# Two decoder layers on one core: routing in two steps, small products in turn, stage seams in quarters

## The chip, the core and the metric

The kernel runs on one core of one Trainium2 chip. A core has five engines, each with its own queue of instructions that it works through in order: TensorE (PE; its loading of the stationary operand is listed apart as PEld), VectorE (DVE), ScalarE (ACT), GpSimd (POOL) and SyncE (SP), which here mostly issues DMAs. They work at the same time and wait for each other through semaphores. TensorE writes to PSUM (banks of 128 x 512 fp32 words); the other data lies in SBUF. The metric is the device time of one execution in microseconds (us), median of several; less is better.

## The reference, cut to what matters

Two consecutive layers of a decoder, one sequence of 256 tokens, width 1024, all in float32:

```
for layer in range(2):
    h = rmsnorm(x, norm1[layer])
    x = x + hybrid_mixer(h, ...)          # proj = h @ w_in; three groups of heads; concat @ w_out
    h = rmsnorm(x, norm2[layer])
    if layer == 0:
        x = x + (silu(h @ ffn_gate) * (h @ ffn_up)) @ ffn_down           # inner width 2816
    else:
        probs = softmax(h @ router)                                      # 8 experts
        top_p, top_i = top_k(probs, 2); top_p /= sum(top_p)
        for e in range(8):
            x += gate[:, e] * swiglu(h, w_gate[e], w_up[e], w_down[e])    # inner width 1536
```

The mixer has three parts side by side: gated DeltaNet (6 heads of 64; a causal convolution, then a recurrence over 4 chunks of 64 tokens that carries a 64 x 64 state per head), forgetting attention (6 heads of 64; softmax attention with a cumulated log decay), and a pooling part of 4 groups with windows of 2 to 16 tokens. In RMSNorm each token is scaled by one positive number, r = 1/sqrt(mean(x^2) + eps), and each channel by a gain.

## The kernel before

**Products.** Every large product is made of three products of fp32r operands: a float32 is split in a high part and the rest, and the sum is hi·hi + hi·lo + lo·hi (`mm3`). `hi_lo` makes the parts: ACT copies the high part (recorded at L238), DVE subtracts (L241). All matmuls are recorded at L244, transposes at their own lines (L361 those of the norm, named `pst`).

**Weights.** `piece` (L283) issues the load of a piece of weights (up to 128 x 1152) on SyncE's queue into a ring of 6 raw buffers (more in the experts' stage), and splits it into one of 4 pairs `whi`, `wlo`. Splits run ahead of their use, as far as these buffers allow. In each stage pieces 2 to 5 are held behind the last split of the norm by a dependency (`self.split_h`), so that the norm's splits come first.

**Stages.** `mixer` of layer 0, `dense`, `mixer` of layer 1, `moe`; a stage begins with `norm` (L346), which multiplies by the gain (`xn`), transposes 8 blocks of 128 x 128 per token tile through four `pst` banks (one pair of PSUM tag F for the first token tile, one of tag D for the second), and splits them into `hThi`, `hTlo`. The factor r isn't applied there: it is worked out beside (four squares on ACT, then Ln, Exp and a Newton step on DVE, buffer `nt`) and multiplied in later. PSUM tags A, D, F have 3, 3, 2 banks in the mixers, 4, 2, 2 in dense, 2, 4, 2 in moe.

**The mixer's small products.** The DeltaNet part makes two Gram matrices per 128 tokens (`gram`, PSUM name `ps_KK`), solves a triangular system (`delta_solve`, `ps_j`), and runs over the four chunks (`delta_scan`): `ps_ks` and `ps_v` for the new values, `ps_S` for the state, and into `ps_o` the output, from the state S (128 x 128 per pair of heads) and from the matrix P (64 x 64 per head). A product of 64 x 64 uses a quarter of the array: the row half by the partitions of its operands (here the chunk), the column half by those of its result. `log_decays` (`ps_c`) turns columns into rows, `attention` sums P·V per head into `ps_fo`.

**The ends of mixer and dense.** The last product of a mixer, `ps_out`, has four quarters (two token tiles by two column halves), each a PSUM bank: three of tag A and then one of tag F. Rows 0 to 4 run as their weights come; rows 5 to 7 are kept, and run quarter by quarter, each followed by its addition to `xs`. In `dense`, a step f makes 128 inner columns of gate and up (`ps_gu`) and adds the down product of the step before (`ps_dn`, four banks); the last two are kept and run quarter by quarter, both of a quarter together, each quarter followed by its addition to `xs` (L975).

**Routing and experts.** `route` (L978) multiplies `hThi`, `hTlo` with the router (`ps_ro`), copies the result (`rt`), folds hi and lo (`ps_lg`), scales by r, forms the softmax, ranks each token's experts by two comparisons with a rule for ties, selects those of rank under 2 (`sel`), and counts each token's place with its expert (`ps_pos`). `experts` (L1109) then fills expert 0's 0/1 matrix `disp` by comparing places with numbers (`fill`), gathers its tokens from `xh` and `xl` (the parts of `xn`, made by ACT and by POOL at L1307) as products with `disp` (`ps_ga`), and goes on to gates, `places` (L1033: the order of the other experts by their load, read by SyncE into registers at L1064, since it sets the address of each load), the other fills, and `slots` (L1090, `ps_slot`: each slot's gate, token and r). Then 32 steps, 8 experts by 4 quarters of the inner width: `gate_up` (`ps_e`), silu with r as its scale (`info`), and one step later `down` (`ps_y`). Three lightly loaded experts ("small") have 64 slots, and their hi and lo parts share one operand; their last two k blocks use the raw float32 weights. `finish` splits an expert's sum, `scatter` adds it to `xs`. `store` issues one DMA per token tile. If an expert overflows its slots, the experts run again for the rest; with these inputs this doesn't happen.

**Order.** The program is written with the Tile framework, whose planner puts each engine's instructions in order by priorities: loads and splits have AHEAD = 2000 over the rest, the norm and the routing twice that. Within an engine the order is then fixed.

Of the kernel before, what the change touches and what calls it, by code (L numbers as in the profile page):

```python
# [16 lines left out]
F32 = mybir.dt.float32  # L17
F32R = mybir.dt.float32r
# [7 lines left out]
D = 1024  # L26
# [59 lines left out]
def shape_constants():  # L86
# [29 lines left out]
    r.add("iota", np.broadcast_to(np.arange(256.0), (128, 256)))  # L116
    r.add("lt", np.broadcast_to((e[None, :] < e[:, None]).reshape(1, 64), (128, 64)))
    r.add("room", np.broadcast_to(np.isin(e, SMALL) * 64.0, (128, 8)))
# [27 lines left out]
def pack(inputs):  # L146
# [30 lines left out]
    out["cst"], out["rcst"] = cst.array(), rcst.array()  # L177
    PAR_AT["cst"], PAR_AT["rcst"] = cst.at, rcst.at
# [8 lines left out]
ORDER = ("x", "gains", "cst", "rcst", "par0", "par1", "win", "wout", "ffn", "moe")  # L187


class Kernel:  # L190
# [92 lines left out]
    def piece(self, ap):  # L283
# [23 lines left out]
    def setup(self):  # L307
# [4 lines left out]
        self.par = [cp.tile([128, self.d[f"par{l}"].shape[1]], F32, name=f"par{l}t") for l in range(2)]  # L312
# [32 lines left out]
    def norm(self, along=True):  # L345
# [7 lines left out]
        for t in range(2):  # L353
# [9 lines left out]
            xn.append(x)  # L363
        ss = self.sm.tile([128, 4], F32, tag="ss", name="ss")
# [6 lines left out]
        nc.vector.tensor_scalar(v, ss[:, 0:2], 1.0 / D, EPS, op0=ALU.mult, op1=ALU.add)  # L371
# [11 lines left out]
        return xn, hi, lo  # L383


    def proj_tokens(self, g, hi, lo):
# [5 lines left out]
        for (k0, k1), (wh, wl) in zip(cuts, ws):  # L392
            for t in range(2):
                tk = slice(t * 128, t * 128 + 128)
                for k in range(k0, k1):
                    s = slice((k - k0) * n, (k - k0 + 1) * n)
                    self.mm3(ps[t][:, :n], hi[:, k, tk], lo[:, k, tk], wh[:, s], wl[:, s], k == 0, k == 7)
# [148 lines left out]
    def delta_keys(self, kq):  # L546
# [42 lines left out]
        for hp in range(3):  # L589
            ps = self.psF("ps_eGb")  # L590
            for t in range(2):
                self.mm(ps[:, t * 128:t * 128 + 128], ex[t][:, 2 * hp:2 * hp + 2].rearrange("p a d -> p (a d)"), self.ident)
            self.copy(eGb[:, hp], ps[:, :T])
# [14 lines left out]
    def gram(self, kq, s, dest, tag):  # L608

        for t in range(2):  # L610
            for h2 in range(2):
                ps = self.ps(tag, "ps_KK")
                r = slice(h2 * 64, h2 * 64 + 64)
                for m in range(3):
                    for c in range(2):
                        n = slice((2 * t + c) * 64, (2 * t + c) * 64 + 64)
# [732 lines left out]
```

## Time and profile before

| | |
|---|---|
| median of 3 runs | 986.93 us (986.68 to 988.48) |
| profiled execution | 987.85 us |
| its span | 986.1 us |
| mean granted TensorE clock | 0.973 |
| moved by DMA | 224.78 MB, mean 228 GB/s |

The span runs from the first to the last instruction in the records; the execution's time has 1.75 us more around it. The stages by their first and last product: mixer 0 to 167.4, dense 171.5 to about 356.6, mixer 1 to 519.5, then routing and experts to the end.

The page gives the busy time of each engine over the span, then the chain that ended last, followed back from the last instruction to whatever released each step. The rows of groups give line, engine, operation, result <- operands by the program's names, partitions x elements and type, and a count; then the busy time, the mean of one in ns, and the idle time of the engine just before them with what ended it. Rows of the timeline start with the time in us from the span's start and the duration; `x4` means four such instructions in a row, taken together. The granted clock (PEclk) is that which the throttle let TensorE have, as a share of full speed. Matmuls overlap: the next starts before the end that is drawn for the last.

### The profile page before, as it was taken

To read this page: it belongs to the slowest core of one execution; us is meant where nothing else is said; L and a number is where in the kernel's file an instruction comes from. 1 tells how busy PE (TensorE), PEld (TensorE's weight loads), DVE (VectorE), ACT (ScalarE), POOL (GpSimd) and SP (SyncE) were. 2 spreads that over 40 slices of the span, in tenths; PEclk is the share of its full clock that TensorE was granted. 3 is DMA by queue.
4 is the path that set the end of the run, shared out by engine and by line. 5 is a ranking of instruction groups with operands and counts; after the bars stand their busy time and mean duration, and the time that the engine had idled before them with its cause. 6 is when DMAs were issued, how large, how long until landed. Compare 5 with 4: busy or idle time off the path is not lost.

```text
span 986.1 us, 17576 instructions
## 1 busy us (share of the span) xinstructions
PE 923.9 (94%) x6483; PEld 823.7 (84%) x6483; DVE 734.8 (75%) x1036; ACT 623.7 (63%) x987; POOL 131.1 (13%) x196
## 2 busy tenths in 40 slices
PE   6988998999999989889994999999999899999996
PEld 6887776999999989788773999987889788998874
DVE  6877657655555568767558587998899898998895
ACT  6754545544444457555535388876887688877773
POOL 2696100000000023881002000000000000000000
PEclk9999999999999989989997799999999999999999
DMA  9533113666666646342134399999999999998991
GB/s 355 169 90 126 45 44 132 213 194 183 187 189 190 174 127 194 107 129 67 41 131 182 98 348 325 364 364 352 374 366 376 358 337 351 391 342 316 330 405 50
DMA packets 61983, 224.78 MB, mean 228 GB/s; under 512 B 6896, under 2 KB 7152, under 8 KB 61888
## 3 DMA queue, kind: packets, MB, share of 16 engines
q1 hardware_dynamic: 61344, 221.62, 64.7%
q0 software_dynamic: 544, 1.94, 0.5%
q8 instruction: 53, 0.87, 0.4%
q14 instruction: 42, 0.34, 0.1%
HBM read 222.49 MB, written 1.05 MB: 227 GB/s over the span
## 4 chain that ended last, share of the span: by engine, by line
PE 75%; DVE 8%; POOL 6%; DMA 5%; ACT 3%; issue 2%; SPq 0%; DVEq 0%; ACTq 0%; POOLq 0%
PE ps_e L244 23%; PE ps_gu L244 13%; PE ps_y L244 11%; PE ps_dn L244 6%; PE ps_out L244 4%; DMA raw<-moe 3%; DVE wlo L241 3%; PE ps_fq L244 3%; PE ps_ga L244 2%; PE ps_o L244 1%; POOL cacc L514 1%; PE ps_p L244 1%; ACT whi L238 1%; POOL U L576 1%; DVE cacc L518 1%
## 5 line engine op out<-in xcount | busy, mean ns | idle before, releaser
L241 DVE TENSOR_TENSOR wlo<-raw,whi 128x1024 fp32r<-128x1024 f32 (+3 forms) x394 | 478.4, 1240 | 138.2 <-ACT whi L238 135.1
L238 ACT ACTIVATE whi<-raw 128x1024 fp32r<-128x1024 f32 (+3 forms) x394 | 412.3, 1066 | 181.2 <-PE ps_e L244 53.7
L244 PE MATMUL ps_e<-wlo,gThi 128*128 128x384 f32 x464 | 161.9, 349 | 4.5 <-DVE wlo L241 4.4
L244 PE MATMUL ps_e<-whi,gThi 128*128 128x384 f32 x464 | 157.8, 346 | 1.2 <-ACT whi L238 1.2
L244 PE MATMUL ps_e<-whi,gTlo 128*128 128x384 f32 x320 | 109.0, 342 | 0.0
L244 PE MATMUL ps_gu<-hThi,whi 128*128 128x256 f32 x352 | 99.1, 282 | 1.3 <-DVE hTlo L241 1.3
L244 PE MATMUL ps_gu<-hTlo,whi 128*128 128x256 f32 x352 | 98.7, 280 | 0.0
L244 PE MATMUL ps_gu<-hThi,wlo 128*128 128x256 f32 x352 | 98.7, 280 | 0.0
L244 PEld LDWEIGHTS ps_e<-wlo,gThi 128*128 128x128 f32 x464 | 89.3, 193 | 9.7 <-DVE wlo L241 6.9
L244 PEld LDWEIGHTS ps_e<-whi,gThi 128*128 128x128 f32 x464 | 88.9, 192 | 4.6 <-ACT whi L238 1.6
L244 PE MATMUL ps_y<-wlo,ehi 128*128 128x512 f32 x192 | 73.4, 401 | 1.0 <-DVE wlo L241 1.0
L244 PEld LDWEIGHTS ps_gu<-hThi,whi 128*128 128x128 f32 x352 | 66.1, 188 | 2.5 <-DVE hTlo L241 1.5
L244 PEld LDWEIGHTS ps_gu<-hThi,wlo 128*128 128x128 f32 x352 | 67.4, 191 | 0.0
L244 PE MATMUL ps_y<-whi,ehi 128*128 128x512 f32 x192 | 65.9, 408 | 1.3 <-DVE ehi L241 1.3
L244 PEld LDWEIGHTS ps_gu<-hTlo,whi 128*128 128x128 f32 x352 | 66.1, 188 | 0.8
L244 PEld LDWEIGHTS ps_e<-whi,gTlo 128*128 128x128 f32 x320 | 61.6, 193 | 0.6
L244 PE MATMUL ps_y<-whi,elo 128*128 128x512 f32 x120 | 46.6, 392 | 0.0
L244 PEld LDWEIGHTS ps_y<-whi,ehi 128*128 128x128 f32 x192 | 36.3, 191 | 9.8 <-DVE ehi L241 2.1
L244 PEld LDWEIGHTS ps_y<-wlo,ehi 128*128 128x128 f32 x192 | 36.2, 190 | 9.3 <-DVE wlo L241 1.8
L244 PE MATMUL ps_e<-raw,gThi 128*128 128x384 f32 x96 | 36.2, 500 | 0.0
L244 PE MATMUL ps_dn<-whi,fhi 128*128 128x512 f32 x88 | 34.4, 391 | 0.1
L244 PE MATMUL ps_dn<-wlo,fhi 128*128 128x512 f32 x88 | 34.3, 389 | 0.0
(394 smaller groups left out, 1794.1 us busy)
## 6 DMA issues: line engine op xcount, KB each, us to landing
raw<-moe SPq DMA_DIRECT2D x128, 576.0 KB, 6.2
raw<-moe SPq DMA_DIRECT2D x96, 512.0 KB, 6.1
raw<-ffn SPq DMA_DIRECT2D x66, 512.0 KB, 3.5
raw<-moe SPq DMA_DIRECT2D x64, 384.0 KB, 5.9
raw<-win SPq DMA_DIRECT2D x34, 512.0 KB, 3.8
raw<-wout SPq DMA_DIRECT2D x16, 512.0 KB, 3.5
raw<-win SPq DMA_DIRECT2D x8, 402.0 KB, 5.1
raw<-win SPq DMA_DIRECT2D x4, 576.0 KB, 4.5
```

The costliest lines, as they stand in the source:

```text
L238: return self.nc.scalar.activation(out, in_, AF.Copy, scale=scale)
L241: return self.nc.vector.tensor_tensor(out, a, b, op=op)
L244: self.nc.tensor.matmul(out, l, r, start=start, stop=stop)
L514: eng.tensor_scalar(acc, x, w[:, o + 3:o + 4], None, op0=ALU.mult)
L518: nc.vector.scalar_tensor_tensor(acc[:, j:], x[:, :T - j], wj, acc[:, j:], op0=ALU.mult, op1=ALU.add)
L576: nc.gpsimd.tensor_tensor(u, u, tv, op=ALU.subtract)
```

## The change

**Routing in two steps.** The order of a token's logits doesn't depend on its r, so the selection now works on the raw logits: one subtraction, one comparison with a constant that holds the rule for ties. r (`factor`), the softmax and expert 0's scale `first` are issued after the products of step 0, the gates (`shares`), `places`, the other fills, `slots` and the parts `xh`, `xl` after those of step 1 (`then`). `xl` moves from POOL to DVE. Expert 0 is gathered from `xn` in float32 and the sum is split (`gather_whole`); its last two k blocks use the float32 operand `g6` and raw weights. `slots` works with fp32r products (6 columns: parts of gate and r, and the token). A table `self.after` says behind what the first five splits of a stage stand: in moe the first two behind the last split of the norm, the next three behind the copy of `rt` (ACT) and the first fill (DVE). The routing's constants are loaded a stage earlier into the buffer of `par0`, by POOL's queue.

```diff
@@ piece
-        if 1 < self.pieces < 6:
-            for i, last in zip(parts, self.split_h):
+        if self.pieces < 6:
+            for i, last in zip(parts, self.after[min(self.pieces, 3)]):
                 self.dep(i, last)
@@ route
-        lg = sm.tile([128, 2, NE], F32, name="lg", bufs=1)
-        self.tt(lg, ps[:, :16].rearrange("p (t e) -> p t e", t=2), self.r[:, :, None].to_broadcast([128, 2, NE]), ALU.mult)
...
+        raw = sm.tile([128, 2, NE], F32, name="lraw", bufs=1)
+        nc.vector.tensor_copy(raw.rearrange("p t e -> p (t e)"), ps[:, :16])
+
         c1 = sm.tile([128, 2, NE, NE], F32, name="c1", bufs=1)
-        c2 = sm.tile([128, 2, NE, NE], F32, name="c2", bufs=1)
-        self.tt(c2, others, mine, ALU.is_equal)
-        self.tt(c1, others, mine, ALU.is_gt)
-        lower = self.rc("lt").rearrange("p (a b) -> p a b", b=NE)[:, None].to_broadcast([128, 2, NE, NE])
-        self.tt(c2, c2, lower, ALU.mult)
-        self.tt(c1, c1, c2, ALU.add)
+        self.tt(c1, raw[:, :, None, :].to_broadcast([128, 2, NE, NE]), raw[:, :, :, None].to_broadcast([128, 2, NE, NE]), ALU.subtract)
+        self.tt(c1, c1, self.rc("tie").rearrange("p (a b) -> p a b", b=NE)[:, None].to_broadcast([128, 2, NE, NE]), ALU.is_gt)
@@ slots
+        for i, v in ((0, gr), (2, r)):
+            nc.vector.tensor_copy(gt[:, :, :, i], v)
+            self.tt(gt[:, :, :, i + 3], v, gt[:, :, :, i].bitcast(F32), ALU.subtract)
...
-                self.mm(ps[:, 3 * e:3 * e + 3], P[t][:, e].bitcast(F32), gt[:, t, e], t == 0, t == 1)
+                self.mm(ps[:, 6 * e:6 * e + 6], P[t][:, e], gt[:, t, e], t == 0, t == 1)
@@ experts
+        def gather_whole():
+
+            g = [self.big.tile([128, 8, 1, 128], F32R, tag=x, name="g" + x) for x in ("Thi", "Tlo")]
+            g.append(wk.tile([128, 2, 128], F32, name="g6", bufs=1))
+            for k in range(0, 8, 4):
+                ps = self.psF("ps_ga")
+                for i in range(4):
+                    for t in range(2):
+                        self.mm(ps[:, i * 128:i * 128 + 128], xn[t][:, (k + i) * 128:(k + i + 1) * 128], P[t][:, 0].bitcast(F32), t == 0, t == 1)
+                self.gathered = self.hi_lo(g[0][:, k:k + 4, 0], g[1][:, k:k + 4, 0], ps.rearrange("p (k c) -> p k c", k=4))
+            self.copy(g[2].rearrange("p k c -> p (k c)"), ps[:, 256:])
+            return g
...
-            self.act(sg, ga, AF.Silu, scale=info[0][:r, p, 2:3])
+            self.act(sg, ga, AF.Silu, scale=first if len(g) == 3 else info[0][:r, p, 2:3])
...
+                self.after[3] = self.rt_copy, filled
+                g[0] = gather_whole()
+
+        def factors():
+
+            nonlocal first
+            begun = self.factor(False)
+            self.dep(begun, self.gathered[1])
+            r2 = wk.tile([128, 2, 2], F32R, name="r2", bufs=1)
+            nc.vector.tensor_copy(r2[:, :, 0], self.r)
+            self.tt(r2[:, :, 1], self.r, r2[:, :, 0].bitcast(F32), ALU.subtract)
+            ps = self.psF("ps_first")
+            for t in range(2):
+                self.mm(ps[:, :2], P[t][:, 0], r2[:, t], t == 0, t == 1)
+            first = wk.tile([128, 1], F32, name="first", bufs=1)
+            self.first_known = nc.vector.tensor_reduce(first, ps[:, :2], axis=AX.X, op=ALU.add)
+            self.softmax()
+            self.tables("silu_and_others")
+
+        def rest_of_routing():
+            nonlocal info
+            begun = [self.shares(), self.places()]
+            fill(slice(1, 6, 2), 128)
...
+            info = self.slots(P)
+            for t in range(2):
+                self.dep(self.hi_lo(xh[t], xl[t], xn[t])[1], self.slots_known)
+            for i in begun:
+                self.dep(i, self.first_known)
```

**Seams.** `proj_tokens` and the first step of `dense` issue all products with `hThi` first, those with `hTlo` after. The quarters of `ps_out` take the banks F, A, A, A instead of A, A, A, F, so that the quarter that closes first holds the bank of tag F. In `dense` the row before the last runs over all four quarters first, then the last one quarter by quarter with the addition to `xs`. The result is stored in four DMAs.

```diff
@@ mixer
-        po = [self.ps("AAAF"[i], f"ps_out{i}") for i in range(4)]
+        po = [self.ps("FAAA"[i], f"ps_out{i}") for i in range(4)]
@@ dense
+        (f0, h0), (f1, h1) = late
         for t in range(2):
             for e in range(2):
-                for f, h in late:
-                    rows(f, t, e, *h)
+                rows(f0, t, e, *h0)
+        for t in range(2):
+            for e in range(2):
+                rows(f1, t, e, *h1)
                 x = self.xs[t][:, e * 512:e * 512 + 512]
```

**Small products in turn.** Products that use different parts of the array are issued alternately: in `gram` over both heads of a pair and both chunks, in `delta_scan` the output products of both chunks of a token tile together (they were issued with each chunk), in `log_decays` over both heads of a pair, in `attention` `ps_fo` once per pair of heads. The three products with the identity for `eGb` become transposes.

```diff
@@ delta_scan
-            for m in range(3):
-                if S is not None:
-                    self.mm(po[r, m * 128:m * 128 + 128], self.qd[:, m, ns], S[:, m], True, False)
-                for h in (2 * m, 2 * m + 1):
-                    self.mm(po[r, h * 64:h * 64 + 64], self.P[r, t * 6 + h], src[r, h], S is None, S is None or h % 2 == 1)
+            states.append(S)
+            if c == 1:
+
+                both = [(c, slice(c * 64, c * 64 + 64), states[2 * t + c]) for c in range(2)]
+                for m in range(3):
+                    for c, r, S0 in both:
+                        if S0 is not None:
+                            ns = slice((2 * t + c) * 64, (2 * t + c) * 64 + 64)
+                            self.mm(po[r, m * 128:m * 128 + 128], self.qd[:, m, ns], S0[:, m], True, False)
+                    for h in (2 * m, 2 * m + 1):
+                        for c, r, S0 in both:
+                            self.mm(po[r, h * 64:h * 64 + 64], self.P[r, t * 6 + h], vt[r, h], S0 is None, S0 is None or h % 2 == 1)
+                done.append(po)
```

More of the change, by code (lines that the diff above doesn't have):

```diff
@@ L363, in norm, with factor @@
             xn.append(x)
+        self.after = {1: (), 2: self.split_h, 3: self.split_h}
+        if along is not None:
+            self.factor(along)
+        return xn, hi, lo
+    def factor(self, along):
+        nc = self.nc
         ss = self.sm.tile([128, 4], F32, tag="ss", name="ss")
@@ L1029, in route, with softmax @@
         self.tt(pos.rearrange("p t e -> p (t e)"), ps[:, :16], sel.rearrange("p t e -> p (t e)"), ALU.mult)
[L1030 to L1031 removed]
+        self.pos, self.counts, self.raw, self.sel = pos, ps, raw, sel
+    def softmax(self):
+        nc, sm = self.nc, self.wk
+        lg = sm.tile([128, 2, NE], F32, name="lg", bufs=1)
+        self.tt(lg, self.raw, self.r[:, :, None].to_broadcast([128, 2, NE]), ALU.mult)
+        mx = sm.tile([128, 2], F32, name="rmx", bufs=1)
+        nc.vector.tensor_reduce(mx, lg, axis=AX.X, op=ALU.max, negate=True)
+        pr = sm.tile([128, 2, NE], F32, name="pr", bufs=1)
+        for t in range(2):
+            self.act(pr[:, t], lg[:, t], AF.Exp, bias=mx[:, t:t + 1])
+        self.pr = pr
@@ L1033, in places, with shares @@
+    def shares(self):
+        nc, sm = self.nc, self.wk
+        gate = sm.tile([128, 2, NE], F32, name="gate")
+        begun = self.tt(gate, self.pr, self.sel, ALU.mult)
+        su = sm.tile([128, 2], F32, name="rsu", bufs=1)
+        nc.vector.tensor_reduce(su, gate, axis=AX.X, op=ALU.add)
+        nc.vector.reciprocal(su, su)
+        self.tt(gate, gate, su[:, :, None].to_broadcast([128, 2, NE]), ALU.mult)
+        self.gate = gate
+        return begun
     def places(self):
         nc, wk = self.nc, self.wk
-        cnt = wk.tile([128, NE], F32, name="cnt", bufs=1)
@@ L1252, in experts @@
                 p, fc = steps[i]
-                if i == 0:
-                    with self.tc.high_priority(offset=2 * AHEAD):
-                        fill(slice(*groups[0]), 128)
-                        g[0] = gather(*groups[0])
-                    if over:
-                        fill(slice(2, NE), 128)
-                    else:
-                        self.gates_of_experts()
-                        self.places()
-                        fill(slice(1, 6, 2), 128)
-                        fill(slice(6, 7), 128)
-                        fill(slice(2, 5, 2), 64)
-                        fill(slice(7, 8), 64)
-                    info = self.slots(P)
-                cur = p, fc, gate_up(p, fc, g[of[p]], p - groups[of[p]][0])
+                then = (factors, rest_of_routing)[i] if i < 2 and not over else None
+                cur = p, fc, gate_up(p, fc, g[of[p]], p - groups[of[p]][0], then)
             if prev is not None:
@@ L1287, in weights @@
             return d[0, fc, :, s, a:b]
-        return d[bass.ds(e, 1), fc, :, s, a:b].rearrange("o p n -> (o p) n")
+        return d[bass.ds(self.order[p], 1), fc, :, s, a:b].rearrange("o p n -> (o p) n")
     def store(self):
         for t in range(2):
-            self.nc.sync.dma_start(self.out[t * 128:(t + 1) * 128], self.xs[t])
+            for i in range(2):
+                c = slice(i * 512, i * 512 + 512)
+                self.nc.sync.dma_start(self.out[t * 128:(t + 1) * 128, c], self.xs[t][:, c])
     def moe(self):
```

204 lines of the change are left out of this document (101 added, 103 removed).

## The prediction, made before the changed kernel had run

> **What bounds the kernel now.** I read the page's engine shares first, then the chain that ended last, then the windows by stage.
>
> ```profile
> PE 923.9 (94%) x6483; PEld 823.7 (84%) x6483; DVE 734.8 (75%) x1036; ACT 623.7 (63%) x987; POOL 131.1 (13%) x196
> PE 75%; DVE 8%; POOL 6%; DMA 5%; ACT 3%; issue 2%; SPq 0%; DVEq 0%; ACTq 0%; POOLq 0%
> 108.00:162.00 54.00, 54.00 (x389) 42.27 (x387) 33.66 (x91) 30.01 (x74) 0.27 (x3) 1.00 0.23 73
> 527.40:538.90 11.50, 0.88 (x9) 0.80 (x9) 10.31 (x28) 4.66 (x10) 5.21 (x2) 0.73 0.41 142
> 538.90:547.10 8.20, 8.14 (x36) 8.17 (x37) 6.20 (x30) 1.20 (x2) 0.00 (x0) 0.50 0.01 2
> 553.40:559.90 6.50, 6.50 (x22) 6.50 (x23) 2.33 (x6) 2.44 (x3) 0.00 (x0) 0.50 0.35 97
> 563.70:956.50 392.80, 385.13 (x2005) 343.07 (x2004) 348.11 (x361) 311.45 (x387) 0.00 (x0) 0.99 0.96 355
> ```
>
> A window row gives stretch, length, then busy time and instruction count of PE, PEld, DVE, ACT, POOL, then granted clock, DMA share and GB/s. TensorE sets the end nearly everywhere. The second half of a mixer (108 to 162) has no idle PE. The experts (563.7 to 956.5) run on a full DMA (0.96), with PE at 385 of 393 us and DVE at 348: three limits close together, so what counts there is when the stream starts. The hole is between: from 527.4 to 538.9 PE works 0.88 us, then runs at half clock (0.50) until the stream is going at 559.9.
>
> The profiled execution took 987.85 us (span 986.1), the runs' median is 986.93; I sum against the former and take 0.9 off at the end. Two runs of this kernel differ by up to 0.2%; that is what I call no change.
>
> **The routing seam.**
>
> ```profile
> 518.67 1.36 DVE L241 TENSOR_TENSOR wlo<-raw,whi 128x1152 fp32r<-128x1152 f32 x1 [2.73 <-ACT whi L238]
> 521.59 2.81 PE L361 MATMUL pst<-cst,xn 128*128 128x128 f32 x16 [2.10 <-DVE xs L241]
> 528.89 5.21 POOL L1307 TENSOR_TENSOR xl<-xn,xh 128x1024 fp32r<-128x1024 f32 x2 [13.83 <-ACT nr L218]
> 529.52 2.30 DVE L241 TENSOR_TENSOR nt<-nv,nr 128x2 f32<-128x2 f32 x1
> 534.15 0.17 DVE L336 TENSOR_SCALAR nt<-nt 128x2 f32<-128x2 f32 x1
> 538.96 0.45 PE L244 MATMUL ps_ga<-disp,xh 128*128 128x128 f32 x1 [0.92 <-DVE disp L241]
> 536.89 0.29 DVE L241 TENSOR_TENSOR c<-c,c 128x128 f32<-128x128 f32 x1
> 550.30 3.87 PE ps_slot L244 x32
> L241 DVE TENSOR_TENSOR xn<-xs,gain 128x512 f32<-128x512 f32 x16 | 10.5, 688 | 7.1 <-DMA gain<-gains 7.0
> L241 DVE TENSOR_TENSOR hTlo<-pst,hThi 128x512 fp32r<-128x512 f32 x16 | 10.5, 687 | 0.8 <-ACT hThi L238 0.7
> L238 ACT ACTIVATE hThi<-pst 128x512 fp32r<-128x512 f32 x16 | 9.1, 595 | 5.0 <-PE pst L361 4.9
> ```
>
> Two DVE operations on 2 elements each stretch to about 2.3 us (529.52, and the next up to 534.15) while POOL's `xl` runs; the one after takes 0.17. The change moves `r` and the softmax off the selection, and `xl` to DVE, behind the slots.
>
> New path to the gather: ps_out ends at 519.5 as now (2.10 us of idle PE before 521.59). The first split of a weight no longer stands ahead of `xs`, and the first token tile's transposes are already done (its PSUM banks are no longer those of the sum that closes last). So, with durations from the grouped rows, xs and xn 0.69 each + four transposes 0.5 (2.81/16 each) + hThi 0.6 + hTlo 0.7 = 522.7; the half of ps_ro that waits for it 1.5, its copy and the fold 1.0 = 525.2; DVE still splits two pieces (2 x 1.36 from 523.3), so the logits are copied at 526.0. Subtract, compare, reduce, select at about 0.3 each, positions 0.7, fill 0.5: the gather starts at about 528.6, not 538.96: **-10.3**. Bounds: -4.5 (only the stretched operations go) to -12.
>
> The gather itself: 32 one-pass products before, 16 two-record f32 ones after, 32 records either way; 0.22 us each now, 7.0 us. f32 records with few columns take 0.12 (3.87/32). I take 0 (-3 to +3).
>
> The slots leave the first step, where they cost 3.87 us and a second cold stretch of 6.5 us at 0.50 (3.25 lost). They return later as 16 single records, 2.0 to 3.5 us. Taken: **-4.5** (-1 to -5).
>
> ```profile
> 643.75 8.15 PE ps_e L244 x47
> 963.60 1.45 PE L244 MATMUL ps_e<-raw,gThi 128*128 128x384 f32 x4
> 964.59 0.92 PE L244 MATMUL ps_y<-whi,ehi 128*128 128x512 f32 x2
> L241 DVE TENSOR_TENSOR wlo<-raw,whi 128x768 fp32r<-128x768 f32 x42 | 40.0, 953 | 3.8 <-ACT whi L238 3.7
> SPq L1064 <- DVE order L1062: 11.2, 1, 11.2
> 533.00:553.00 20.00, 14.32 (x78) 14.26 (x77) 12.99 (x55) 4.32 (x8) 1.10 (x1) 0.58 0.02 7
> ```
>
> Expert 0's last two k go raw: 0.50 us each (four records in 0.99) against three products at 0.173 (8.15/47); no gain on PE, but eight splits of 0.95 go from DVE. That pays for what is deferred: places, fills, slots and gates (6.2 us of DVE between 538.9 and 547.1), `r` (1) and the two `xl` (2.5), some 10 us, which now fall among the splits of steps 0 to 2, on an engine without the old waiting time to do them in. By the row of 563.7 to 956.5, 31 steps, a step lasts 12.7 us and holds 11.2 of DVE, for expert 0 now 9.3; with the head start of four split pieces most fits: I charge **+2** (0 to +10). Squares and the table load run on ACT beside the same matmuls. The rest of the stage then moves as a block, because the DMA, idle from 533 to 553 (share 0.02) with ring and split buffers full, restarts when the first pieces are consumed: near 541. Seam together: **-12.8**.
>
> The new waits. The first two splits now stand behind the last hThi and hTlo, splits 3 to 5 behind the logits' copy on ACT and the first fill on DVE; behind them in both queues stand only later splits, for which PE waits after the gather, 7 us on: no cost. The first silu waits for `first`, that is for `r` through a small product that PE reaches after step 0. Behind it on ACT stand step 1's splits; PE goes on meanwhile, since four PSUM banks hold the sums of two steps. If `r` came later than the end of step 0, each us would cost one; its chain (four squares, Ln, Exp, some small DVE operations) runs beside 10 us of step 0. The constants come by POOL's queue, one set a stage ahead: no cost.
>
> On the clock: PE busy from 538.9 to 547.1, mostly with the gather, did not lift it from 0.50, so I keep a cold gather and some 4 us of cold ps_e, as now.
>
> The Trainium skill, "TensorE: Matmul & The Clock Gate", Part 1, lets the full clock return after about 3.4 us of sustained work. By that rule the old gather would have ended warm; this trace disagrees.
>
> **The other seams.**
>
> ```profile
> 153.41 8.45 PE ps_out L244 x36
> 168.27 1.94 PE L361 MATMUL pst<-cst,xn 128*128 128x128 f32 x16 [0.87 <-DVE xs L241]
> 171.51 0.38 PE L244 MATMUL ps_gu<-hThi,whi 128*128 128x256 f32 x1 [1.30 <-DVE hTlo L241]
> 355.97 2.73 DVE L975 SCALAR_TENSOR_TENSOR xs<-ps_dn,nr,xs 128x512 f32<-128x512 f32 x4 [2.00 <-PE ps_dn L244]
> 359.44 3.65 PE L361 MATMUL pst<-cst,xn 128*128 128x128 f32 x16 [2.82 <-DVE xn L241]
> 358.80:365.30 6.50, 5.86 (x24) 5.86 (x25) 6.20 (x14) 4.91 (x12) 3.40 (x6) 0.50 0.21 76
> 977.57 2.62 SPq L1292 DMA_DIRECT2D out<-xs  x2
> ```
>
> Mixer 0 to dense: all 16 transposes wait for the last `xs`, and the first ps_gu for hTlo. Half the transposes go early and hi products go first: from 167.4 (168.27 - 0.87) only xs, xn, four transposes and hThi remain (2.5 us), start 170.1: **-1.4** (0 to -2). Dense to mixer 1: four `xs` come in one block, then PE idles 2.8 us and runs 6.5 us at 0.50. The last ps_dn thus ends at 356.6. Closing each quarter after its own three products (0.235 each, 8.45/36) closes the first 9 products earlier, so `xs` starts near 354.5 and the transposes near 356; the DVE chain of eight 0.68 us operations then ends 1.5 earlier, and part of the 3.25 lost to the cold clock returns: **-2.5** (0 to -6). The store goes in four pieces instead of two: from the second issue (about 980.2) to the span's end 5.9 us pass, and the last piece has half the bytes: **-0.5** (0 to -1.5).
>
> **Small products in turn.**
>
> ```profile
> 98.08 1.95 PE ps_j L244 x128
> 117.06 0.91 PE L244 MATMUL ps_v<-V,U 64*64 64x64 f32 x12
> 117.89 0.86 PE L244 MATMUL ps_fo<-PT,fv 128*64 128x256 f32 x4
> 118.69 0.55 PE L812 MATMUL ps_pt<-cst,Pf 128*128 128x128 f32 x3
> 119.99 0.56 PE L244 MATMUL ps_S<-vt,Kd 64*64 64x64 f32 x12
> 120.39 0.39 PE L244 MATMUL ps_o<-vt,P 64*64 64x64 f32 x4
> 120.72 0.43 PE L244 MATMUL ps_o<-S,qd 128*64 128x128 f32 x2
> 121.08 0.44 PE L244 MATMUL ps_o<-vt,P 64*64 64x64 f32 x4
> 93.77 1.40 PE ps_c L244 x12
> ```
>
> A record's end is drawn some 0.2 us after the next may start, so I take start to next start. ps_v, all in one part of the array, needs 0.83 us for 12 records (0.069); ps_S, whose heads alternate between two column halves, 0.40 (0.033). So turns halve a run. Per layer, by records: ps_o from P 48 at up to 0.092 (4.1 us, to 1.6), ps_o from S 18 at 0.18 (12 of them pair: -1.1), ps_fo 24 at 0.20 (-2.4), ps_c 24 at 0.117 (-1.4): 7.4 a layer. The grams alternate columns already, and the transposes for eGb stand early, where PE isn't full: I count nothing for these. I take half, **-7.5** for both layers (0 to -15): what is late next is the scan, whose matmuls wait in turn for DVE and ACT copies.
>
> One caution: the P products of two chunks come from different row halves of the array and end in one PSUM bank. So do the four quarters of ps_j, 128 records in 1.95 us, 0.015 each against 0.033 for the larger ps_S; they overlap.
>
> The Trainium skill, "TensorEngine Tiling (Array Packing)", Gotcha 1, says that different row tiles cannot use the same PSUM bank at the same time. By that rule ps_j could not overlap; the trace speaks against it.
>
> **Sum:** 987.85 - 12.8 - 1.4 - 2.5 - 0.5 - 7.5 = 963.15, less 0.9: **962 us**.
>
> **Rivals.**
> 1. Turns give nothing, because the order written isn't the one executed or the time saved is spent waiting for the scan's copies: 962 + 7.5 = 969.5. For: many of these runs are short and stand between others; against: no idle PE in 108 to 162. 0.14. A smaller form: only the P pairs, one bank from two row halves, wait for each other; that takes back half of 2.5 us in each layer: 964.5. 0.03. That is the Trainium skill's Gotcha 1 at work.
> 2. The deferred routing isn't covered: PE stands in expert 0 until fills and slots are done, its 10 us in full: 962 + 8 = 970. For: DVE is busy 348 of 393 us in this stage; against: eight splits fewer. 0.15.
> 3. The heads of the norm still queue behind splits, as an in-order planner may place them; the seams keep only the removed operations: gather at 534.5, other seams 0: 962 + 6 + 4 = 972. 0.08.
> 4. The f32 gather, two records for each product, does lift the clock: half of 4 us of cold ps_e and 1 us of gather saved: 959. For: the gap ahead of it is a third as long; against: the row of 538.9 to 547.1. 0.07. That is the Trainium skill's clock rule at work.
> 5. **Slower than before.** SyncE reads the experts' order from DVE in its queue; that read held it 11.2 us before, harmlessly, as the ring was full. Now the order needs `first_known`. If the read stands ahead of expert 0's remaining loads, DMA starts only when the order stands. Forecast restart is 541; each us later is one of idle DMA. Orders known after 541 + 25 = 566 make the kernel slower; known at 575, behind step 1's splits: 962 + 34 = 996. Against: expert 0's loads need no register, and the read can be placed behind them. 0.04.
>
> The forecast keeps 0.49. Range: down to 951 for most of the mixers' full 15 us and the warm gather, up to 977 for two of rivals 1 to 3 partly together. All but rival 5 end more than 2 us below 986.93: faster 0.94, same 0.02, slower 0.04.
>
> **What would show it.** In the profile after: first ps_ga near 529 instead of 538.96, no 2.3 us `nt`; DMA share high from 541; a PE gap in expert 0 if the routing isn't covered; ps_o's P records at 0.035 to 0.045 us apart; pst starting before the last `xs` at each seam, and the 0.50 stretch at 359 shorter. Wrong would be: SyncE's wait on `order` with DMA idle behind it, or mixers of the old length.

## The result, and the profile after

The changed kernel takes **972.8 us** (median of 4 runs, 967.22 to 976.07) beside 986.8 for the kernel before (4 runs, 986.46 to 988.48): ratio 0.985, 95% interval 0.980 to 0.990. The forecast was 962 with a range of 951 to 977: the sign and the range held, but the gain is 14 us instead of 25. The profiled execution took 973.49 us (span 971.6, mean granted clock 0.978).

The page's engine shares and the shares of its chain, of the kernel after:

```profile
PE 916.2 (94%) x6441; PEld 807.4 (83%) x6441; DVE 724.8 (75%) x1030; ACT 616.8 (63%) x978; POOL 125.5 (13%) x195
PE 69%; DVE 9%; POOL 7%; DMA 6%; ACT 5%; issue 4%; SPq 0%; ACTq 0%; DVEq 0%; POOLq 0%
```

The shares look as before; 14 us can't be found in them. So I cut both spans at the same events, mostly first or last products, and compare piece by piece, one execution of each kernel:

| stretch | before, us | after, us | difference | forecast |
|---|---|---|---|---|
| start of the span to the first transposes | 7.73 | 6.94 | -0.8 | 0 |
| mixer 0, to the end of ps_out | 159.67 | 157.73 | -1.9 | (1) |
| then to the first ps_gu | 4.11 | 4.11 | 0 | -1.4 |
| dense, to the end of ps_dn | 185.1 | 185.1 | 0 | 0 |
| then to mixer 1's first weights (`zabf`) | 6.12 | 4.96 | -1.2 | -2.5 |
| mixer 1, to the end of ps_out | 156.75 | 154.63 | -2.1 | (1) |
| then to the first ps_ga | 19.47 | 9.64 | **-9.8** | -10.3 |
| gather to the end | 447.11 | 448.55 | **+1.4** | -3.0 |

(1) -7.5 for both mixers. Not every row is clear of chance. The changed kernel profiled once more (`after_again`, below) has 159.5 and 152.4 us for the mixers instead of 157.7 and 154.6, and `b_turns`, which leaves the last stage as it was before, has 444.0 us there instead of 447.1. The routing's row is clear of it: 19.0 to 19.5 us in the four profiles with the old routing, 9.64 to 9.66 in three with the new one. The differences add to the span's 14.4; the forecast's terms make 24.7. Three places miss: the mixers by 3.4, the two early seams by 2.7, and the experts' stage by 4.4.

The windows of the kernel after (stretch, length, busy time and count of PE, PEld, DVE, ACT and POOL, granted clock, DMA share, GB/s):

```profile
108.00:160.00 52.00, 51.12 (x397) 39.34 (x391) 34.41 (x93) 29.96 (x77) 0.27 (x3) 1.00 0.27 82
522.60:526.00 3.40, 2.93 (x14) 2.96 (x15) 3.03 (x4) 2.92 (x9) 0.00 (x0) 0.50 0.68 175
526.00:529.40 3.40, 3.40 (x28) 3.40 (x28) 1.14 (x2) 1.20 (x2) 0.00 (x0) 1.00 0.81 289
542.80:569.80 27.00, 23.26 (x110) 18.74 (x109) 21.55 (x49) 12.76 (x14) 0.00 (x0) 0.94 0.69 233
569.80:950.50 380.70, 372.79 (x1918) 326.99 (x1917) 334.33 (x347) 298.08 (x374) 0.00 (x0) 1.00 0.95 352
```

The same steps of the kernel before, as two windows:

```profile
108.00:160.00 52.00, 52.00 (x379) 40.70 (x378) 31.86 (x85) 29.53 (x74) 0.27 (x3) 1.00 0.22 70
584.40:965.80 381.40, 373.24 (x1929) 330.05 (x1928) 337.93 (x351) 301.14 (x378) 0.00 (x0) 0.99 0.95 353
```

Three things are to be seen. A mixer's second half now shows 0.9 us of idle PE between 108 and 160, where there was none. But 0.67 of that is a wait for `ohi` that the kernel before has as well, just past the end of the window (first before, then after):

```profile
162.86 0.50 PE L244 MATMUL ps_out<-whi,ohi 128*128 128x512 f32 x1 [0.67 <-ACT ohi L238]
```

```profile
159.51 0.50 PE L249 MATMUL ps_out<-whi,ohi 128*128 128x512 f32 x1 [0.67 <-ACT ohi L243]
```

The half clock behind the gather lasts only 3.4 us. And the experts' stage differs only in its first three steps: from the third `ehh` (each step's inner result, made by DVE) to the last but one, 381.40 us became 380.70. The kernel after reaches the first two `ehh` 21 us ahead of before, and the third only 14.6 ahead (569.78 against 584.40). From the first `ehh` to the third, 542.8 to 569.8, PE stands 3.7 us; in the kernel before it doesn't stand at all there (563.75 to 584.40). That is where part of the experts' term went.

### The profile page after: what moved, and what is told of

It reads as the page before. It is cut to its first block, busy times and chain, and to the rows that moved or that the text cites. A ratio compares the mean times of both kernels' runs of the same rounds, so it can differ in the third digit from the quotient of the medians.

```text
span 971.6 us, 17466 instructions
## 1 busy us (share of the span) xinstructions
PE 916.2 (94%) x6441; PEld 807.4 (83%) x6441; DVE 724.8 (75%) x1030; ACT 616.8 (63%) x978; POOL 125.5 (13%) x195
## 4 chain that ended last, share of the span: by engine, by line
PE 69%; DVE 9%; POOL 7%; DMA 6%; ACT 5%; issue 4%; SPq 0%; ACTq 0%; DVEq 0%; POOLq 0%
PE ps_e L249 21%; PE ps_gu L249 13%; PE ps_y L249 10%; PE ps_dn L249 6%; PE ps_out L249 5%; DMA raw<-moe 4%; DVE wlo L246 3%; ACT whi L243 3%; PE ps_fq L249 2%; PE ps_ga L249 1%; POOL U L591 1%; POOL tmp L589 1%; PE ps_p L249 1%; PE ps_q L249 1%; PE ps_v L249 1%
## 5 line engine op out<-in xcount | busy, mean ns | idle before, releaser
L246 DVE TENSOR_TENSOR wlo<-raw,whi 128x1024 fp32r<-128x1024 f32 (+3 forms) x386 | 471.3, 1245 | 125.7 <-ACT whi L243 119.8
L243 ACT ACTIVATE whi<-raw 128x1024 fp32r<-128x1024 f32 (+3 forms) x386 | 405.8, 1072 | 178.6 <-PE ps_e L249 42.7
L249 PE MATMUL ps_e<-wlo,gThi 128*128 128x384 f32 x448 | 155.4, 347 | 6.7 <-DVE wlo L246 6.5
L249 PE MATMUL ps_e<-whi,gThi 128*128 128x384 f32 x448 | 152.5, 345 | 1.5 <-ACT whi L243 1.5
L249 PE MATMUL ps_e<-whi,gTlo 128*128 128x384 f32 x304 | 102.5, 339 | 0.0
L249 PE MATMUL ps_gu<-hTlo,whi 128*128 128x256 f32 x352 | 96.4, 280 | 0.0
L249 PEld LDWEIGHTS ps_e<-wlo,gThi 128*128 128x128 f32 x448 | 84.8, 189 | 13.4 <-DVE wlo L246 10.2
L249 PEld LDWEIGHTS ps_e<-whi,gThi 128*128 128x128 f32 x448 | 84.4, 189 | 6.6 <-ACT whi L243 2.9
L249 PE MATMUL ps_y<-whi,ehi 128*128 128x512 f32 x192 | 67.9, 415 | 1.5 <-DVE ehi L246 1.3
L249 PEld LDWEIGHTS ps_e<-whi,gTlo 128*128 128x128 f32 x304 | 57.3, 189 | 0.9
```

What stands on the lines that cost most here:

```text
L243: return self.nc.scalar.activation(out, in_, AF.Copy, scale=scale)
L246: return self.nc.vector.tensor_tensor(out, a, b, op=op)
L249: self.nc.tensor.matmul(out, l, r, start=start, stop=stop)
```

## The experiments

**Which part brings what.** Four kernels. `b_turns` has the products in turn alone (`gram`, `delta_scan`, `log_decays`, `attention` and the transposes for `eGb`), `b_seams` the seams alone (`proj_tokens`, the banks, `dense`, the store), both on the kernel before; `r_only` undoes both in the kernel after, so it keeps the routing alone. `b_gather32` gives the kernel before the float32 gather and nothing else of the routing:

```diff
-                        g[0] = gather(*groups[0])
+                        g[0] = gather(*groups[0]) if over else gather_whole()
```

Expected of `b_turns`:

> The kernel before with the mixers' small products in turn alone (gram, delta_scan, log_decays, attention, transposes for eGb). The prediction took 7.5 off for both layers: 979. Against it: mixer 0 from its first product to its end is 1.95 shorter in the changed kernel and mixer 1 2.1, other edits among them, so 983. If PE only waits for the scan's copies instead: 986.8. In each case mixer 0 (first product to the end of ps_out, 159.7 before) and mixer 1 (zabf to ps_out, 156.8) shorten by half of it each.

Expected of `b_seams`:

> The kernel before with the seams alone (hi products first, quarters in the banks F, A, A, A, dense's last row quarter by quarter, four stores). The prediction took 1.4 + 2.5 + 0.5 off: 982.4. Against it: in the changed kernel the first transposes of dense start 0.87 behind the last ps_out as before, behind the last addition to xs, so 0 at that seam, and about 1.5 at dense to mixer 1: 985. The transposes' start tells it: 166.5 or earlier by the prediction, 168.3 by the other.

Expected of `b_gather32`:

> The kernel before with expert 0 gathered from xn in float32 and split behind it, as the changed kernel does, everything ahead of it and the idle gap (528 to 538) as before. Theory F (the form of the operands lifts the clock): the granted clock is full within 4 us of the gather's start, and the time falls by 3 to 4, to 983. Theory G (the length of the gap ahead of it, 0.69 us instead of 7.9 behind ps_lg, kept the chip warm in the changed kernel): 0.50 until about 549 as before, 986 to 988.

Expected of `r_only`:

> The two-step routing alone on the kernel before: turns and seams undone. If the parts add up: the whole change (1.5% below before) less the turns (0.4%) and less the seams (0 to 0.25%): 0.85 to 1.1% below before, some 8.5 to 11 us. From the end of ps_out to ps_ro 4.15, to the gather another 5.5, as in the whole change.

| kernel | median, us | kernel before beside it | ratio, 95% interval |
|---|---|---|---|
| b_turns | 979.3 | 983.5 | 0.996 (0.994 to 0.998) |
| b_seams | 981.54 | 983.5 | 0.9975 (0.995 to 0.9999) |
| b_gather32 | 980.54 | 983.5 | 0.9974 (0.9954 to 0.9994) |
| r_only | 979.05 | 984.58 | 0.995 (0.9926 to 0.9974) |

The three parts alone add to -1.15%, the whole is -1.5% with an interval that includes it: no hidden interaction is needed. By the ratios the routing alone gains 4.9 us (2.6 to 7.3), the seams 2.5 (0.1 to 4.9) and the turns 3.9 (2.1 to 5.9). `r_only` thus missed its expectation of 8.5 to 11 us, although its stretch from ps_out to the gather came out as expected (4.16 and 5.50 us). The seams' gain is barely clear of nothing. In the profile of `b_seams` the first ps_gu starts 4.11 us behind ps_out, as before; 0.6 us less stands between dense and mixer 1, and 0.6 behind the last addition.

The timeline of `b_turns` shows how the turns do it, on PE (start, duration, x records):

```profile
150.07 0.44 PE L244 MATMUL ps_o<-S,qd 128*64 128x128 f32 x4
150.44 0.45 PE L244 MATMUL ps_o<-vt,P 64*64 64x64 f32 x8
150.82 0.44 PE L244 MATMUL ps_o<-S,qd 128*64 128x128 f32 x4
```

Four P records took 0.33 to 0.37 us before (120.39 to 120.72, 121.08 to 121.45); eight take 0.38 now, two row halves of the array in one PSUM bank. Four S records take the 0.37 of two. So the records do overlap as counted, and the small form of rival 1 falls. The two mixers as windows, first of the kernel before, then of `b_turns`:

```profile
7.73:167.40 159.67, 150.27 (x1452) 130.02 (x1452) 113.16 (x215) 94.76 (x213) 59.01 (x88) 0.99 0.40 133
362.74:519.49 156.75, 147.96 (x1438) 128.62 (x1436) 107.07 (x203) 89.53 (x199) 57.31 (x87) 0.97 0.38 120
```

```profile
7.26:164.26 157.00, 149.04 (x1446) 128.45 (x1446) 112.28 (x215) 94.77 (x213) 59.82 (x88) 0.97 0.41 136
359.65:513.58 153.93, 143.64 (x1432) 124.51 (x1430) 105.99 (x203) 89.43 (x199) 58.53 (x87) 0.97 0.39 122
```

Together they are 5.5 us shorter. PE is idle as long as before (18.2 us in both kernels), so what the records free doesn't turn to waits. But it works longer at half clock: 20.5 us of the mixers in this trace, 13.0 before. Counting half of PE's busy time there as lost, I estimate that PE was spared some 9 of the 15 us, and that the clock took some 3.7 of these back. The runs say the same: the mean granted clock of the 12 runs of `b_turns` is 0.972, that of the 29 runs of the kernel before beside them 0.976. Why the clock is lower, and where the rest of the 15 us is, no run shows.

**The clock behind the gather.** First `b_gather32`, then `b_turns`, which gathers as before, as windows from about the gather's start (535.51 and 532.82):

```profile
535.00:540.00 5.00, 4.49 (x21) 4.52 (x22) 4.81 (x27) 0.27 (x1) 0.00 (x0) 0.50 0.02 3
540.00:545.00 5.00, 5.00 (x41) 5.00 (x41) 2.49 (x10) 0.92 (x2) 0.00 (x0) 0.91 0.00 0
```

```profile
532.80:544.00 11.20, 11.18 (x46) 11.20 (x47) 6.86 (x31) 1.65 (x3) 0.00 (x0) 0.50 0.01 1
```

Both have the long gap ahead of the gather. With fp32r products PE is as good as fully busy and stays at 0.50 for 11.2 us: through the gather, which ends at about 541.2 with four ps_e in between, and some 3 us into the ps_e behind it. With float32 ones it is at full speed 5.4 us after the start, still within the gather. The form of the gather's products decides, not the gap: rival 4 is right, and the stretch from gather to end is 441.6 us in `b_gather32`, against 447.1, 444.0 and 443.7 in three profiles with the old gather (before, `b_turns`, `b_seams`; the last has 0.6 less from its store).

The kernel after, which has the same gather, takes 448.55, `after_again` (the same kernel once more) 447.9 and `r_only` 449.7. So by these profiles deferring the rest of the routing makes the stage 6 to 8 us longer than the new gather alone. The forecast had it 2.5 us shorter: -4.5 for the slots that leave the first step, +2 for what returns. Of the -4.5, 3.25 was for a second half-clock stretch behind the slots; `b_gather32`, whose slots are still there (from 542.4), has none:

```profile
545.00:560.00 15.00, 15.00 (x92) 14.96 (x92) 11.42 (x14) 10.59 (x13) 0.00 (x0) 1.00 0.58 198
```

**What PE waits for in the third step.** In the kernel after, first ACT's high-part copies, then PE's rows with a wait and the two that follow it:

```profile
538.77 1.06 ACT L243 ACTIVATE whi<-raw 128x1024 fp32r<-128x1024 f32 x1
540.34 1.06 ACT L243 ACTIVATE whi<-raw 128x1024 fp32r<-128x1024 f32 x1 [0.50 <-PE ps_e L249]
543.41 1.06 ACT L243 ACTIVATE whi<-raw 128x1024 fp32r<-128x1024 f32 x1 [1.03 <-PE ps_e L249]
544.98 1.16 ACT L243 ACTIVATE whi<-raw 128x1152 fp32r<-128x1152 f32 x1 [0.50 <-PE ps_e L249]
549.28 1.16 ACT L243 ACTIVATE whi<-raw 128x1152 fp32r<-128x1152 f32 x1 [3.14 <-PE ps_e L249]
554.72 1.16 ACT L243 ACTIVATE whi<-raw 128x1152 fp32r<-128x1152 f32 x1 [4.27 <-PE ps_e L249]
```

```profile
547.59 0.44 PE L249 MATMUL ps_e<-wlo,gThi 128*128 128x384 f32 x1 [0.95 <-DVE wlo L246]
550.50 0.44 PE L249 MATMUL ps_e<-whi,gThi 128*128 128x384 f32 x1 [1.25 <-ACT whi L243]
552.46 0.44 PE L249 MATMUL ps_e<-wlo,gThi 128*128 128x384 f32 x1 [1.52 <-DVE wlo L246]
556.47 2.27 PE L249 MATMUL ps_slot<-gt,disp 128*128 128x6 f32 x16
558.59 0.55 PE L1252 MATMUL ps_ht<-cst,ehh 128*128 128x128 f32 x3
```

The pieces of 128 x 1024 are those of expert 0's first `down`, three of them, split by 544.5 into three of the four pairs `whi`, `wlo`. But PE's order has the third step's gate and up products and the slots ahead of that `down` (ps_ht, 558.59). The gate's pieces (1152) must share the one pair that is left: ACT waits 3.14 and 4.27 us for PE to free it, PE 0.95 + 1.25 + 1.52 for ACT and DVE, and a short cold stretch follows. (`after_again` has the same 3.74 us of idle PE there and no cold stretch; it takes 25.4 us from the first to the third `ehh` instead of 27.0.) I put `rest_of_routing` behind the first or the second `down` instead, so that PE frees the pairs first:

```diff
-                then = (factors, rest_of_routing)[i] if i < 2 and not over else None
+                then = factors if i == 0 and not over else None
...
                 down(p, fc, hh, py)
+                if i == 1 and not over:
+                    rest_of_routing()
```

(`a_late`: `i == 2`.)

> The changed kernel with one edit: the rest of the routing is issued behind the down products of step 0 instead of ahead of them. Theory O (order: in the changed kernel three of the four pairs whi/wlo hold the weights of step 0's down from 538.8 to 561, while PE stands at step 2's gate with the one pair that is left, so that loads stop between 548 and 564): DMA share between 545 and 570 rises from about 0.7 to over 0.9, and the time falls by 5 to 9, to 964 to 967. Theory D (the ten us of deferred routing on DVE are the limit, wherever they stand): no change, 971 to 975. Theory S (the hole closes, but the stream of weights is the bound behind it, so little of it reaches the end): 968 to 971.

> The rest of the routing one step later still, behind the down products of step 1. The order of the experts is then known some 12 to 15 us later than in the changed kernel (547.6), while SyncE issues the first load that needs it at 565.6. Rival 5 of the prediction gives each us behind that time one us of idle DMA: order at 560 to 563, no loss by it; and if DVE's deferred work is better spread, 1 to 2 less than with the rest behind step 0's down. If the read stands ahead of loads that don't need it, DMA is idle from 550 to the read, and the time is 5 to 10 longer.

From the first to the third `ehh`, `a_down_first` in a window:

```profile
543.20:565.60 22.40, 20.58 (x104) 16.81 (x103) 19.81 (x48) 12.49 (x13) 0.00 (x0) 1.00 0.86 302
```

and `a_late`:

```profile
541.70:562.50 20.80, 19.47 (x93) 15.98 (x92) 18.03 (x42) 11.74 (x13) 0.00 (x0) 1.00 0.85 296
```

The stretch falls from 27.0 to 22.4 and 20.8 us, idle PE from 3.74 to 1.82 and 1.33, the clock stays at 1.00 and the DMA share rises from 0.69 to 0.86. Part of it returns when the deferred work runs later: from the gather to the sixth `ehh` it is 88.2 in the kernel after, 85.7 and 84.3 in these. So the order is the cause of some 2.5 to 4 us of that stretch. Against the 82.2 us of `b_gather32` another 2 to 3.5 remain, whose cause is open. In the times it can't be told apart: `a_down_first` 971.53 us, ratio 0.986 (0.983 to 0.989), `a_late` 970.05, 0.985 (0.981 to 0.989). The 964 to 967 us of theory O did not come; 971.53 is a time of theory D, and what speaks for O is the stretch alone.

**The raw products of expert 0.** In the kernel after a group with its raw part takes longer than three split products for each k:

```profile
533.68 1.45 PE L249 MATMUL ps_e<-raw,g 128*128 128x384 f32 x4
534.67 0.63 PE L249 MATMUL ps_e<-whi,gTlo 128*128 128x384 f32 x1
535.14 0.34 PE L249 MATMUL ps_e<-whi,gThi 128*128 128x384 f32 x1
```

From 533.68 to 535.14, less the 0.17 of one split product, is 1.29 us for four raw records; six products at 0.173 make 1.04. That is 2 us over eight groups, which the forecast had at nothing. Two kernels undo it:

```diff
-                    if (small or len(g) == 3) and k1 == 8:
+                    if small and k1 == 8:
...
```

> The changed kernel with expert 0's last two k blocks split like the others (no g6, no raw weights in expert 0). Theory R (a raw group of two float32 products holds PE about 1.3 us, from its start to the start of the second product behind it, against 1.04 for six single products of 0.173, eight times): 2 less between the gather and the sixth ehh (88.2 in the changed kernel, 86 expected), and 1 to 2 less in time. Theory V (eight more splits, 7.6 us of DVE, fall into the stretch in which DVE also does the deferred routing, and PE waits for splits there already): 90 or more, and 2 or more slower.

> The same edit on the version with one PSUM pool and the rest of the routing behind step 0's down products, where PE waited 2.6 us for splits in that stretch. By R 2 less than that version (85.5 from the gather to the sixth ehh, some 964); by V 2 more (968).

It gained nothing: `a_no_raw` takes 976.57 us, ratio 0.9915 (0.988 to 0.995), and 90.4 us from gather to sixth `ehh` instead of 88.2, with 5.8 us of idle PE there instead of 3.7 (1.9 of them before the slots, for `gt` from DVE) and 13.6 us at half clock instead of 6.4. On `a_pool_down` (below) that stretch is 0.8 shorter than with raw products (85.6 against 86.4), but the time is 971.97, 0.987 (0.983 to 0.991), against 966.28. Both medians are worse, though the intervals overlap with those of the kernels that they vary. Both also ran at a lower clock: 0.974 as the mean of the runs against 0.981 and 0.983 for `after` and `after_again`, and 0.977 against 0.983. By these means they spent some 15 and 11 us more at half clock; half of it, lost, would be about 7 and 6 us (an estimate), and the medians differ by 4 to 6 and by 5.7. So undoing the raw products doesn't help, but that the spared splits are the reason is not shown: the lower clock alone could make the difference.

**Why the early seams gained nothing.** PE's timeline of the kernel after, at the three seams:

```profile
165.54 1.94 PE L366 MATMUL pst<-cst,xn 128*128 128x128 f32 x16 [0.87 <-DVE xs L246]
168.78 0.39 PE L249 MATMUL ps_gu<-hThi,whi 128*128 128x256 f32 x1 [1.30 <-DVE hTlo L246]
...
352.77 1.07 PE L249 MATMUL ps_dn<-whi,flo 128*128 128x512 f32 x4
356.67 2.37 PE L366 MATMUL pst<-cst,xn 128*128 128x128 f32 x16 [2.83 <-DVE xn L246]
...
514.30 1.94 PE L366 MATMUL pst<-cst,xn 128*128 128x128 f32 x16 [0.87 <-DVE xs L246]
517.58 0.30 PE L249 MATMUL ps_ro<-hTlo,rw 128*32 128x256 f32 x1 [1.35 <-DVE hTlo L246]
522.12 0.17 PE L249 MATMUL ps_pos<-sel,Ub 128*128 128x8 bf16 x1 [1.44 <-DVE sel L1049]
523.07 5.22 PE L249 MATMUL ps_ga<-disp,xn 128*128 128x128 f32 x32 [0.69 <-DVE disp L246]
```

and the end of dense in the kernel before:

```profile
355.55 1.08 PE L244 MATMUL ps_dn<-whi,flo 128*128 128x512 f32 x4
```

At 165.54 and 514.30 all 16 transposes still wait for the last `xs`, as before, though the bank that they need closed first. My reading: each stage opens a PSUM pool of its own, and the pool is given back as a whole. At the end of dense the planner had already put the four whi·flo products last; all quarters closed together before, and they do after, in 1.07 us. `a_one_pool` keeps one pool for the first three stages:

```diff
+        three = ExitStack()
+        k.pp = three.enter_context(tc.tile_pool(name="mix_ps", bufs=1, space=PSUM))
...
-        po = [self.psA(f"ps_dn{i}") for i in range(4)]
+        po = [self.ps("FAAA"[i], f"ps_dn{i}") for i in range(4)]
```

> The changed kernel with one PSUM pool for mixer 0, dense and mixer 1 (three, three and two banks; ps_dn in banks F, A, A, A) instead of one for each. Theory P (a stage's PSUM pool is given back as a whole, so that the first transposes of the next stage wait for the last addition to xs, whichever bank it reads): the first token tile's transposes stand among the last products of ps_out, the first ps_gu starts 2.7 behind the end of ps_out instead of 4.11, and the time falls by 1 to 2. At dense to mixer 1 nothing changes, since the four quarters of ps_dn close together there. Theory Q (the chain behind the last addition sets the start, whatever the transposes do): 4.11 as before, and the same time.

Its timeline at the first seam:

```profile
164.66 0.39 PE L249 MATMUL ps_out<-whi,olo 128*128 128x512 f32 x1
164.96 0.66 PE L366 MATMUL pst<-cst,xn 128*128 128x128 f32 x4
166.56 0.66 PE L366 MATMUL pst<-cst,xn 128*128 128x128 f32 x4 [0.94 <-DVE xn L246]
166.97 0.37 PE L249 MATMUL ps_gu<-hThi,whi 128*128 128x256 f32 x1
```

Half the transposes now run among the last ps_out, and ps_gu starts 1.92 us behind them instead of 4.11: the pool, with the banks dealt alike on both sides of the border, was the wait. Its time shows no gain, though: 975.0 us, ratio 0.9913 (0.9885 to 0.994). In its profile mixer 1 takes 158.2 us instead of 154.63, with as much time at half clock as the kernel after (17.4 and 17.1 us) and 2.2 us more of idle PE; why isn't shown.

**Both mended.** `a_pool_down` has one PSUM pool for all four stages (every fourth ps_e in a bank of tag A) and `rest_of_routing` behind the first `down`; `a_pool_late` has it behind the second. `after_again` is the changed kernel itself once more, beside `a_pool_down`:

```diff
-         "dense": {"A": 4, "D": 2, "F": 2}, "all": {"A": 2, "D": 4, "F": 2}}
+         "dense": {"A": 3, "D": 3, "F": 2}, "all": {"A": 3, "D": 3, "F": 2}}
...
-                ps = self.psD("ps_e")
+                self.turn = (self.turn + 1) % 4
+                ps = self.ps("DDDA"[self.turn], "ps_e")
```

> The changed kernel, unchanged, as the measure for its variants on the same chip: 967 to 976 as before; the stretch from the end of ps_out to the first ps_gu 4.11, from the last ps_out of mixer 1 to ps_ro 4.15.

> One PSUM pool for all four stages (moe with three, three and two banks as well, every fourth ps_e in a bank of A), and the rest of the routing behind the down products of step 0. By theory P 1.4 less at the first seam and 1.2 to 1.5 less between the last ps_out and ps_ro; by theory O 2 to 3 less behind the gather. Together 4 to 6 below after_again. If the third bank for ps_e in A is in the way of ps_y, the experts get longer (ehh of the last step more than 425 behind the gather).

> The two edits that shortened their stretches, together: one PSUM pool for all stages, and the rest of the routing behind the down products of step 1. If they add up: 1.92 from ps_out to ps_gu, 2.11 from the last ps_out to ps_ro, 84 to 85 from the gather to the sixth ehh (88.2 in the changed kernel), and 1.9 to 2.3% below before, 962 to 967. If the weight stream is the bound from there on, the stretch behind the gather gains, and the end doesn't: 966 to 970.

`a_pool_down` takes **966.28 us** (964.19 to 968.39), ratio 0.982 (0.979 to 0.986); `after_again` 970.53 (967.68 to 975.24), 0.987 (0.983 to 0.991). That is 4.2 us less by the medians, though the intervals overlap. By its profile the seams (ps_out to ps_gu, and to ps_ro) fall from 4.11 and 4.15 to 1.92 and 2.11 us, but only the first is kept whole: from ps_ro to the gather it takes 6.69 instead of 5.49. `a_pool_late`, 968.52 (965.37 to 970.31), 0.984 (0.981 to 0.987), gives no more. No kernel of the study was shown to be faster than `a_pool_down`.

## Why the prediction was right, and where it was wrong

**The routing seam, -10.3: right.** Measured -9.8, and `r_only` has 528.41 - 518.75 = 9.7 us from the end of ps_out to the gather, like the kernel after, without the other parts. The two splits that I let DVE make ahead of the logits' copy stood there, 2.63 us. One detail failed: the first tile's transposes are not done early (514.30), so the half of ps_ro that waits starts 4.15 us behind ps_out, where the forecast had 3.2 (522.7). That is a loss of one microsecond at most.

**The gather's clock, "I keep a cold gather and some 4 us of cold ps_e": wrong**, and in the kernel's favour. I read from a busy fp32r gather that no gather lifts the clock; `b_gather32` shows that a float32 one does. It stood as rival 4 with a chance of 0.07 and 3 us; alone it is worth 2.6 us (0.6 to 4.5).

**The deferred routing, +2 "most fits": this step failed**, and it made the largest miss. The sum was by engine: so much DVE work into so much DVE time. The stall came from an order: three of four split pairs were held for a `down` that PE reaches only after the third step's gate and the slots. It is rival 2's outcome (routing not covered) by another mechanism: 27.0 us from first to third `ehh`, 3.7 of them idle PE, against 22.4 and 20.8 when the routing stands behind a `down`. That explains 2.5 to 4 of the 6 to 8 us; the rest is open. The slots' own price was right: 16 records in 2.1 us (556.47 to 558.59; estimate 2.0 to 3.5). The raw products cost 2 us where I had taken nothing, but undoing them doesn't help. Gather to end thus gained the clock and lost more: +1.4 for -3.0. By one profile of each, that is -5.5 for the gather (forecast 0) and +6.9 for the deferred routing (forecast -2.5, and -0.5 for the store). The two errors partly cancel, and that the time still fell in the range owes something to luck.

**Early seams, -1.4 and -2.5: the first is 0, the second is not the change's.** "The first token tile's transposes are already done" rested on the banks; the pool, not the bank, is what the next stage waits for. "Closing each quarter after its own three products" had no effect, because the order executed already differed from the one written, as the timeline before could have told me (355.55, x4). The 1.2 us gained there come with a cold stretch that is missing after (mean clock 0.50 from 358.8 to 365.3 before), not with the sums: `b_gather32`, without the edit, has 5.31 us there with 1.0 us at half clock, `b_seams`, with it, 5.56 with 1.6. Why the stretch is missing isn't shown. The store's -0.5 is right: from the last addition to the end 5.48 us instead of 6.25.

**Turns, -7.5: right mechanism, size off.** `b_turns` measured -3.9 (-5.9 to -2.1), about a quarter of the records counted. I halved that count for the scan's waits, but PE waits no longer than before. Its profile shows some 9 us less work for PE (my estimate above), of which the clock took back some 3.7. The sum had no term for the clock of the mixers.

**"Two runs of this kernel differ by up to 0.2%": too little.** That came from three runs. The 73 runs of the kernel before beside the experiments go from 977.0 to 990.0 us, with medians from 983.4 to 984.8, and the longer ones mostly have the lower granted clock. The 986.8 beside the changed kernel lies above these medians; `after_again`, beside 21 of these runs, has a ratio of 0.987 instead of 0.985.

**Rival 5** wasn't tested: the read of the order stayed early in `a_late`, so its price remains open. So does the place of the remaining savings in the mixers.

## What to carry to other kernels

When work is moved behind another step, don't only add up engine times: list which buffers of a small ring are already taken, by whom, and when the engine that frees them gets there in its own order. Before a seam is rewritten, look in the trace for the order that is executed and for what the next stage truly waits for; here a pool given back as a whole cancelled a change of banks. And judge each part by a kernel that has only that part, and look at the clock before a difference is put down to waits: the whole was a forecast half right, the parts show the routing seam right and three steps that weren't.

## What the runs showed of the hardware

The clock's return depends on what TensorE runs. In the three kernels that gather with 128 x 128 fp32r products (before, `b_turns`, `b_seams`) it stays at 0.50 for 10.8 to 11.7 us from the gather's start, which is all of the gather and the first ps_e behind it. With float32 products it stays there for 2.9 and 5.4 us (the kernel after, `b_gather32`). The Trainium skill, "TensorE: Matmul & The Clock Gate", Part 1, lets it return after about 3.4 us of sustained work: the kernel after agrees (522.6 to 526.0), the fp32r gathers do not (in the kernel before, PE runs nothing but the gather from 538.96 to 544.1). What in the form of the products decides, the runs don't tell.

Products from two row halves into one PSUM bank overlap: eight in 0.38 us, where four took 0.33 to 0.37. The Trainium skill, "TensorEngine Tiling (Array Packing)", Gotcha 1, excludes that; the measurement decides. Here each row half writes 64 partitions of its own in the bank; products into the same ones weren't measured.
